# The MLP's down projection as 2x2 blocks with seven block products, with two weight sums made in DRAM

## The chip, the cores and the metric

The kernel runs on one core of a Trainium2 chip. The metric is the device time of one execution in microseconds, from the first instruction to the end. The profile's span is the time from the first to the last instruction of one profiled execution.

## The reference

One layer of an encoder on 512 tokens of width 2048, all in float32. Its last step is the one that changes:

```python
h = x
xn = rmsnorm(h);  y = xn @ W_in
h += concat[gdn(y[:, :4112]), rwkv7(y[:, 4112:])] @ W_out   # 8 heads x 128, 16 heads x 64
h += cross_attention(rmsnorm(h), rmsnorm(mem))              # 4 heads, 256 memory tokens
h += (max(rmsnorm(h) @ W_up, 0) ** 2) @ W_down              # 2048 -> 8192 -> 2048
out = rmsnorm_final(h)
```

## The kernel before

Activations are kept transposed: channels on the 128 partitions, the 512 tokens along the free axis. `hres[n]` (n = 0 to 15) is the residual's tile of 128 channels x 512 tokens. A float32 product is made of three fast ones: an operand x is split into `hi`, x rounded by a cast on ScalarE (ACT, L130), and `lo` = x - `hi` on VectorE (DVE, L131), and hi x hi, hi x lo and lo x hi are added up in PSUM. So each weight tile of 128x1024 is loaded by SP's queue (`wraw`), cast by ACT (`whi`), subtracted by DVE (`wlo`) and used by 24 matmuls on TensorE (PE).

The stages in order: the input projection (`py`), head pair by head pair, with the two recurrences of each pair (RWKV-7 tiles have names such as `ri`, `rs`; GDN tiles `gi`, `gs`); the output projection; the cross attention (`kp`, `vp`, `kq`, `vo`, `sc`, `at`, `op`); up; down; the last normalisation.

GpSimd (POOL) works in the first part only. For each pair of heads it inverts small triangular matrices by substitution, one diagonal at a time, in two chains: `sr` for RWKV-7 (64 partitions, from a MEMSET of `sr` to a COPY of `sr`) and `sgi`/`sgj` for GDN (32 partitions, to a COPY of `sgi`). SP's queue stores each result to DRAM (`bg16T<-sr`, `bg8T<-sgi`) and reads it back in another layout (`r`, `E`, `gk`, `gqn`). The same queue, in the same order, loads the projection's weights (`wraw<-in_w_in`).

The order of the first part is set by a scheduler in the program: operations of the projection and of the recurrences (whose line in the profile is L247) are merged by estimated times. The order in each engine's queue is fixed when the kernel is built, and each engine and each queue issues in order. An instruction that waits holds up what stands behind it.

Up (W_up, 2048 x 8192) is computed in 32 steps `p` as 2x2 blocks with seven block products each (Strassen's scheme in Winograd's form) in place of eight. The activations' seven combinations (`comb`, tiles `cb_`) are made once ahead of it. Each step loads four weight tiles, makes four weight sums on DVE, and has seven products of 24 matmuls with 256 columns (half the tokens). The sums of products are made on DVE (L1438). `square` (L1537, L1538) applies the squared ReLU; two transfers per step, issued by ACT, put the result u into DRAM (`Ud`).

Down (W_down, 8192 x 2048) is plain: eight slabs `e` of 1024 rows of W_down; for each slab 16 output tiles `n`, each with one weight tile and 24 matmuls of 512 columns, `dn`, added into `hres[n]` by DVE (L1559). Pieces of u are read back (`usplit`) and split one slab ahead. The last slab goes by halves of the tokens (`last`), so that the normalisation of the first half runs beside the products of the second; `scaled` (L1583) multiplies and stores.

Of the kernel before, what the change touches and what calls it, by code (L numbers as in the profile page):

```python
# [73 lines left out]
def build(tc, I, out):  # L74
# [267 lines left out]
    VOd = [pd.tile([P, 8, 512], F32, name=f"vod{i}", tag=f"vod{i}") for i in range(4)]  # L342

# [881 lines left out]
    hres = [ph.tile([P, T], F32, tag=f"h{k}", name=f"h{k}", bufs=1) for k in range(16)]  # L1225
# [159 lines left out]
    def put(i, k, src):  # L1385
        t = comb[i][k]
        S.copy(t[:, HA], src)
        V.tensor_tensor(out=t[:, HB], in0=src, in1=t[:, HA].bitcast(F32), op=ALU.subtract)

    def sub(o, a, b):  # L1390
        V.tensor_tensor(out=o, in0=a, in1=b, op=ALU.subtract)

    def place(i, k, e, o):


        if i == T1:
            sub(e[:, HA], e[:, HB], e[:, HA])
        elif i == T2:
            sub(e[:, HA], o[:, HB], e[:, HA])
        elif i == T3:  # L1400
            sub(e[:, HB], o[:, HB], e[:, HB])
        elif i == T4:
            sub(e[:, HA], e[:, HA], o[:, HA])
        put(i, k, o[:, HB] if i == B22 else o[:, HA] if i == B21 else e[:, HB] if i == T3 else e[:, HA])

    def strassen(nm, pool, src, ks, done, used=None, first=False):

        w = len(ks) * P

        def raw(p_, tag, bufs, i):
            cnt[0] += 1
            r = p_.tile([P, 1024], F32, tag=tag, name=f"{tag}_{cnt[0]}", bufs=bufs)[:, 0:w] \
                if p_ is pw else p_.tile([P, pool[1]], F32, tag=tag, name=f"{tag}_{cnt[0]}", bufs=bufs)[:, 0:w]
            if i is not None:
                nc.sync.dma_start(r, src[i])
            return r

        def product(i, tag, a):
            cnt[0] += 1
            hi = pw.tile([P, 1024], F32R, tag="whi", name=f"whi{cnt[0]}", bufs=NWS)[:, 0:w]
            lo = pw.tile([P, 1024], F32R, tag="wlo", name=f"wlo{cnt[0]}", bufs=NWS)[:, 0:w]
            split(a, hi, lo)
            pt = psb(f"{nm}_{i}", tag)[:, 0:M]
            for z, k in enumerate(ks):
                sl = slice(z * P, z * P + P)
                mm(pt, hi[:, sl], comb[i][k][:, HA], start=z == 0, stop=False)
                mm(pt, hi[:, sl], comb[i][k][:, HB], start=False, stop=False)  # L1430
            for z, k in enumerate(ks):
                mm(pt, lo[:, z * P:z * P + P], comb[i][k][:, HA], start=False, stop=z == len(ks) - 1)
            if used:
                used(i)
            return pt

        def add(o, a, b, op=ALU.add):
            V.tensor_tensor(out=o, in0=a, in1=b, op=op)  # L1438

        def wraw2(i):  # L1440
            return raw(pool[0], "wraw2", 3, i)

        def ws():
            return raw(pool[0], "ws", 2, None)

        a11 = raw(pw, "wraw", NWR, 0)
        if first:
            a12, a22 = raw(pw, "wraw", NWR, 3), raw(pw, "wraw", NWR, 2)
            a21 = wraw2(1)
        else:  # L1450
            a21 = raw(pw, "wraw", NWR, 1)
            a22, a12 = wraw2(2), wraw2(3)
        p1 = product(B11, "mx", a11)
        c1 = sl2()
        c11, c12 = u1, u4 = c1[:, HA], c1[:, HB]
        S.copy(u1, p1)
        if first:
            p2 = product(B21, "mg", a12)
            p4 = product(T4, "mx", a22)
        s1 = ws()  # L1460
        add(s1, a21, a22)
        p5 = product(T1, "mg", s1)
        s2 = ws()
        add(s2, s1, a11, ALU.subtract)
        p6 = product(T2, "mm", s2)
        c2 = sl2()
        c21, c22 = u3, u2 = c2[:, HA], c2[:, HB]
        add(u2, u1, p6)
        if first:
            add(c11, u1, p2)  # L1470
        add(u4, u2, p5)
        add(a21, a11, a21, ALU.subtract)
        p7 = product(T3, "mm", a21)
        add(u3, u2, p7)
        add(c22, u3, p5)
        done(1, HB, c2)
        if not first:
            p4 = product(T4, "mx", a22)
        add(c21, u3, p4, ALU.subtract)
        done(1, HA, c2)  # L1480
        s4 = ws()
        add(s4, a12, s2, ALU.subtract)
        p3 = product(B22, "mg", s4)
        add(c12, u4, p3)
        done(0, HB, c1)
        if not first:
            p2 = product(B21, "mm", a12)
            add(c11, u1, p2)
        done(0, HA, c1)
# [3 lines left out]
    for n in range(KD):  # L1493
# [9 lines left out]
        if n % 2 == 0 and n < KD - 2:  # L1503
            for i in (B11, T1):
                place(i, n // 2, ge, None)
        elif n % 2 == 1:
            for i in range(2, 7) if n < KD - 2 else (B11, T1, B21, T2, T4, T3, B22):
                place(i, n // 2, ge, g)
# [3 lines left out]
    Ud = [pd.tile([P, 2, 512], F32, name=f"ud{i}", tag=f"ud{i}") for i in range(32)]  # L1512
    pu_cm = tc.tile_pool(name="pu", bufs=1, reuse_waits="tile")
    pu = pu_cm.__enter__()
    uhl = [], []

    def usplit(f):
        if f >= 8:
            r = sl2()
        elif f % 2:  # L1520
            r = ph.tile([P, T], F32, tag="acc", name=f"ur{f}", bufs=1)
        else:
            r = pu.tile([P, T], F32, tag="ur", name=f"ur{f}", bufs=1)
        nc.sync.dma_start(r, Ud[f // 2][:, f % 2, :])
        hi, lo = act_tile(f"uh{f}"), act_tile(f"ul{f}")
        if f < 56:
            split(r, hi, lo)
        else:
            for t, half in ((hi, HA), (lo, HB)):
                split(r[:, half], t[:, HA], t[:, HB])  # L1530
        uhl[0].append(hi)
        uhl[1].append(lo)

    for p in range(32):
        def square(i, half, c):
            t = c[:, half]
            V.scalar_tensor_tensor(out=t, in0=t, scalar=0.0, in1=rstd[:, half], op0=ALU.max, op1=ALU.mult)  # L1537
            S.activation(t, t, AF.Square)  # L1538
            if half is HA:
                nc.scalar.dma_start(Ud[p][:, i, :], c)  # L1540

        def used(i):
            if p == 0 and i == B21:
                pt = psb("pss2")
                mm(pt, ones, acc)
                rsq(rstd, pt, 1.0 / 2048, b_eps6)
            if p == 31 and i in (T1, T2, T3):
                for f in (range(0, 3), range(3, 6), range(6, 8))[i - T1]:
                    usplit(f)

        strassen(f"up{p}", (pu, 1024), [I["w_up"][p, i] for i in range(4)], list(range(8)), square, used, p == 0)
    for e in range(7):
        uh, ul = uhl[0][e * 8:], uhl[1][e * 8:]
        for n in range(KD):
            if n % 2 == 0:
                usplit(e * 8 + 8 + n // 2)
            pt = psb(f"dn{e}_{n}", "mm", 2)
            gemm(pt, I["w_dn"][e, n], 8, uh, ul)
            V.tensor_tensor(out=hres[n], in0=hres[n], in1=pt, op=ALU.add)  # L1559


    def last(n, half, wide):

        pt = psb(f"dn7_{n}", "mm", 2)
        wh, wl = wload(I["w_dn"][7, n])
        u = uhl[half is HB][56:]
        h = hres[n][:, half]
        for k in range(8):
            sl = slice(k * P, k * P + P)
            if wide:  # L1570
                mm(pt, wh[:, sl], u[k], start=k == 0, stop=False)
            else:
                mm(pt[:, HA], wh[:, sl], u[k][:, HA], start=k == 0, stop=False)
                mm(pt[:, HA], wh[:, sl], u[k][:, HB], start=False, stop=False)
            mm(pt[:, HA], wl[:, sl], u[k][:, HA], start=False, stop=k == 7)
        V.tensor_tensor(out=h, in0=h, in1=pt[:, HA], op=ALU.add)
        if wide:
            V.tensor_tensor(out=h, in0=h, in1=pt[:, HB], op=ALU.add)

    acc = ph.tile([P, T], F32, tag="acc", name="acc3", bufs=1)  # L1580
# [6 lines left out]
    ready = []  # L1587
    for half in (HA, HB):
        for n in range(KD):
            last(n, half, half is HA or n < KD - 1)  # L1590
            sq = acc[:, half] if n == 0 else sl2(M)
            S.activation(sq, hres[n][:, half], AF.Square)
            if 0 < n < KD - 1:
                V.tensor_tensor(out=acc[:, half], in0=acc[:, half], in1=sq, op=ALU.add)
            for _ in range(2 if 1 < n < 5 else n > 1):
                if ready:
                    scaled(ready.pop(0), HA)
        pt = psb("pss3")[:, HA]
# [108 lines left out]
```

## Time and profile before

| | us |
|---|---|
| median of 3 runs (range) | 3058.04 (3057.87 to 3059.95) |
| span of the profiled execution | 3053.3 |
| the median above that span | 4.7 |
| PE busy | 3022.5 |
| PEld (weight loads of PE, beside it) busy | 2607.5 |
| DVE busy | 1916.1 |
| ACT busy | 1355.4 |
| POOL busy | 216.3 |

The page does not give the profiled execution's whole time, only its span; the median of the runs stands for it. The DMA queues moved 403.14 MB, 132 GB/s as a mean. In rows of the profile, L12 is a line of the kernel, `out<-in` are the names of tiles without their numbers, and what stands in brackets behind a row, or behind an arrow, is what ended the wait ahead of it. SPq and ACTq are transfers issued by SP and ACT.

### The profile page before, as it was taken

To read this page: it belongs to the slowest core of one execution; us is meant where nothing else is said; L and a number is where in the kernel's file an instruction comes from. 1 tells how busy PE (TensorE), PEld (TensorE's weight loads), DVE (VectorE), ACT (ScalarE), POOL (GpSimd) and SP (SyncE) were. 2 spreads that over 40 slices of the span, in tenths; PEclk is the share of its full clock that TensorE was granted. 3 is DMA by queue.
4 is the path that set the end of the run, shared out by engine and by line. 5 is a ranking of instruction groups with operands and counts; after the bars stand their busy time and mean duration, and the time that the engine had idled before them with its cause. 6 is when DMAs were issued, how large, how long until landed. Compare 5 with 4: busy or idle time off the path is not lost.

```text
span 3053.3 us, 50831 instructions
## 1 busy us (share of the span) xinstructions
PE 3022.5 (99%) x20740; PEld 2607.5 (85%) x20740; DVE 1916.1 (63%) x2881; ACT 1355.4 (44%) x1864; POOL 216.3 (7%) x547
## 2 busy tenths in 40 slices
PE   9999999999999999999999999999999999999998
PEld 7888878878878898778878999999999888888887
DVE  7666666666677647534348888888887443444457
ACT  6455455455555555533336544444444222222234
POOL 0312311312312000000000000000000000000000
PEclk9999999999999999999999999999999999999999
DMA  5322322323425586753323433333334332333335
GB/s 186 104 80 80 108 80 80 108 80 87 135 73 162 172 272 231 262 201 122 110 92 90 142 130 130 132 132 135 125 135 163 124 118 104 125 125 125 113 130 180
DMA packets 226746, 403.14 MB, mean 132 GB/s; under 512 B 91656, under 2 KB 115468, under 8 KB 226512
## 3 DMA queue, kind: packets, MB, share of 16 engines
q1 hardware_dynamic: 210384, 372.62, 37.5%
q10 hardware_dynamic: 16128, 27.27, 2.4%
q8 instruction: 163, 2.67, 0.3%
q14 instruction: 71, 0.58, 0.1%
HBM read 352.23 MB, written 47.59 MB: 131 GB/s over the span
## 4 chain that ended last, share of the span: by engine, by line
PE 95%; DVE 1%; ACT 1%; DMA 1%; issue 1%; POOL 0%; SPq 0%; DVEq 0%; ACTq 0%; POOLq 0%
PE dn L122 23%; PE up L122 21%; PE py L247 21%; PE op L122 6%; PE vp L122 3%; PE sc L122 3%; PE at L122 3%; PE kq L247 3%; PE vo L122 3%; PE kp L247 2%; PE rs L247 1%; PE gs L247 1%; PE pgB L247 1%; PE po L247 0%; PE gpo L247 0%
## 5 line engine op out<-in xcount | busy, mean ns | idle before, releaser
L130 ACT CAST whi<-wraw 128x1024 fp32r<-128x1024 f32 x384 | 403.6, 1051 | 814.3 <-PE dn L122 474.8
L131 DVE TENSOR_TENSOR wlo<-wraw,whi 128x1024 fp32r<-128x1024 f32 x384 | 469.7, 1223 | 135.6 <-ACT whi L130 131.5
L122 PE MATMUL up<-cb,whi 128*128 128x256 f32 x3584 | 467.4, 283 | 1.3 <-ACT whi L130 0.7
L122 PEld LDWEIGHTS up<-cb,whi 128*128 128x128 f32 x3584 | 446.3, 192 | 2.4 <-ACT whi L130 1.7
L122 PE MATMUL dn<-ul,whi 128*128 128x512 f32 (+1 forms) x1032 | 395.0, 389 | 0.9 <-ACT whi L130 0.9
L122 PE MATMUL dn<-uh,whi 128*128 128x512 f32 x1024 | 393.8, 390 | 0.0
L122 PE MATMUL dn<-uh,wlo 128*128 128x512 f32 (+1 forms) x1024 | 384.5, 375 | 0.0
L247 PE MATMUL py<-xhi,whi 128*128 128x512 f32 x928 | 371.8, 401 | 6.1 <-ACT xhi L247 6.0
L247 PE MATMUL py<-xhi,wlo 128*128 128x512 f32 x928 | 371.7, 401 | 0.0
L247 PE MATMUL py<-xlo,whi 128*128 128x512 f32 x928 | 371.4, 400 | 0.3 <-DVE xlo L247 0.3
L247 DVE TENSOR_TENSOR wlo<-wraw,whi 128x1024 fp32r<-128x1024 f32 (+1 forms) x180 | 221.7, 1231 | 128.2 <-ACT whi L247 126.5
L1559 DVE TENSOR_TENSOR h<-h,dn 128x512 f32<-128x512 f32 x112 | 77.0, 688 | 331.1 <-PE dn L122 331.1
L247 ACT CAST whi<-wraw 128x1024 fp32r<-128x1024 f32 (+1 forms) x180 | 188.2, 1046 | 203.0 <-PE py L247 165.3
L122 PE MATMUL up<-cb,wlo 128*128 128x256 f32 x1792 | 251.5, 283 | 0.0
L122 PEld LDWEIGHTS up<-cb,wlo 128*128 128x128 f32 x1792 | 231.2, 192 | 0.0
L122 PEld LDWEIGHTS dn<-ul,whi 128*128 128x128 f32 x1032 | 193.9, 188 | 41.2 <-ACT whi L130 1.2
L122 PEld LDWEIGHTS dn<-uh,whi 128*128 128x128 f32 x1024 | 192.2, 188 | 40.9
L122 PEld LDWEIGHTS dn<-uh,wlo 128*128 128x128 f32 x1024 | 192.3, 188 | 35.0
L247 PEld LDWEIGHTS py<-xhi,whi 128*128 128x128 f32 x928 | 174.9, 188 | 41.2 <-ACT xhi L247 6.2
L247 PEld LDWEIGHTS py<-xlo,whi 128*128 128x128 f32 x928 | 174.9, 188 | 35.6 <-DVE xlo L247 1.4
L247 PEld LDWEIGHTS py<-xhi,wlo 128*128 128x128 f32 x928 | 174.9, 189 | 35.3 <-issue 1.0
L130 ACT CAST whi<-ws 128x1024 fp32r<-128x1024 f32 x96 | 100.5, 1047 | 150.8 <-PE up L122 93.9
(741 smaller groups left out, 5145.4 us busy)
## 6 DMA issues: line engine op xcount, KB each, us to landing
wraw<-in_w_dn SPq DMA_DIRECT2D x144, 512.0 KB, 3.5
wraw<-in_w_up SPq DMA_DIRECT2D x128, 512.0 KB, 3.5
wraw<-in_w_in SPq DMA_DIRECT2D x116, 512.0 KB, 3.6
wraw<-in_wk SPq DMA_DIRECT2D x32, 512.0 KB, 3.9
wraw<-in_wqT SPq DMA_DIRECT2D x32, 512.0 KB, 5.4
wraw<-in_wv SPq DMA_DIRECT2D x32, 512.0 KB, 4.6
wraw<-in_wo SPq DMA_DIRECT2D x32, 512.0 KB, 5.9
wraw<-in_w_out SPq DMA_DIRECT2D x32, 512.0 KB, 3.9
```

The source lines that it names most:

```text
L122: PE.matmul(o, l, r, start=start, stop=stop)
L130: S.copy(hi, src)
L131: V.tensor_tensor(out=lo, in0=src, in1=hi.bitcast(F32), op=ALU.subtract)
L247: f(*a, **k)
L1559: V.tensor_tensor(out=hres[n], in0=hres[n], in1=pt, op=ALU.add)
```

## The change

Down is now computed with seven block products too. W_down is cut into four chunks `c` of 2048 rows, each a 2x2 of blocks: A11, A21, A22, A12 for each pair of output tiles. Each chunk computes one product at a time over all eight half tiles `m`; a product's block is 24 matmuls of 256 columns (`block`, L1436 and L1439). Partial sums that two outputs share stay in PSUM: `X[a]` takes products 0, 3, 5 and 6, `y` products 2 and 4, and `z` product 1; `into` adds them, 512 columns at a time, into the residual, which now lies in tiles `hq`.

Up writes, in place of u, its seven combinations: u's four blocks and three differences, with four transfers per step into `Cd`. Up's own sums of products are partly made in PSUM now, with the signs of some combinations turned. `piece_` reads a piece of a combination back and splits it.

Of the weight sums that down needs, two (T2's and B22's) are made on DVE in SBUF. The other two, S1 = A22 + A21 and S3 = A11 + A21, are made in DRAM (`SUMS`): for each of 16 tiles, a GpSimd transfer copies one block (1.05 MB), and a second one adds the other to it as it writes. That is 64 transfers of 1.05 MB each, DRAM to DRAM. 224 weight tiles are loaded in down, 144 before.

The core of the diff:

```diff
+    SUMS = {i: [pd.tile([P, 2048], F32, name=f"ws{i}_{u}", tag=f"ws{i}_{u}") for u in range(16)] for i in (0, 1)}
+    Cd = [pd.tile([P, 7, 512], F32, name=f"cd{q}", tag=f"cd{q}") for q in range(16)]
...
+    for u in range(16):
+        for i, b in ((0, 2), (1, 0)):
+            GP.dma_start(SUMS[i][u], I["w_dn"][u, b])
+            GP.dma_start(SUMS[i][u], I["w_dn"][u, 1], accum_op=ALU.add, max_dma_last_dim=2048)
...
+    def block(pt, a, parts, start):
...
+        split(a, hi, lo)
+        for k in range(8):
+            for x in parts[k]:
+                PE.matmul(pt, hi[:, k * P:k * P + P], x, start=start, stop=False, skip_group_check=True)
+                start = False
+        for k in range(8):
+            PE.matmul(pt, lo[:, k * P:k * P + P], parts[k][0], start=False, stop=k == 7, skip_group_check=True)
...
         def used(i):
-            if p == 0 and i == B21:
-                pt = psb("pss2")
+            if p == 0 and i == T1:
+                pt = psb("pss2", "scr", 1)
                 mm(pt, ones, acc)
                 rsq(rstd, pt, 1.0 / 2048, b_eps6)
...
+        nc.scalar.dma_start(Cd[p // 2][:, 2:4, h], v(c2))
+        nc.scalar.dma_start(Cd[p // 2][:, 0:2, h], v(c1))
+        nc.scalar.dma_start(Cd[p // 2][:, 4:6, h], v(t))
+        nc.scalar.dma_start(Cd[p // 2][:, 6, h], t4)
...
-    for e in range(7):
-        uh, ul = uhl[0][e * 8:], uhl[1][e * 8:]
-        for n in range(KD):
-            if n % 2 == 0:
-                usplit(e * 8 + 8 + n // 2)
-            pt = psb(f"dn{e}_{n}", "mm", 2)
-            gemm(pt, I["w_dn"][e, n], 8, uh, ul)
-            V.tensor_tensor(out=hres[n], in0=hres[n], in1=pt, op=ALU.add)
...
+        for a in range(4):
+            y = psb(f"dy{c}_{a}", *TAGS[a])
+            ms = (2 * a, 2 * a + 1)
+            s1 = [raw(weights(c, m, S1)) for m in ms]
+            for m in ms:
+                down(c, 2, m, y, s1[m % 2], True)
+            into(a, OD, HB, y, ADD)
+            a11 = [raw(weights(c, m, A11)) for m in ms]
+            for m in ms:
+                add(s1[m % 2], s1[m % 2], a11[m % 2])
+                down(c, 3, m, X[a], s1[m % 2], False)
+            into(a, EV, HB, X[a], SUB)
...
+        for m in range(8):
+            down(c, 5, m, X[m // 2], raw(weights(c, m, S3)), False)
+            if m % 2:
+                into(m // 2, OD, HB, X[m // 2], ADD)
```

Where the sums in DRAM stand on POOL: at its start. Before the change its first memsets (`WTz`, `BTz`, `TtG`) were followed by the chain on `sr`:

```order
L247 MEMSET BTz 128x896
L247 MEMSET TtG 128x512
L247 MEMSET sr_980 64x256
L247 MEMSET sr_980 64x16
L247 ISA
L247 TENSOR_TENSOR gEs_1025<-gE_764,cst 128x512
L247 TENSOR_TENSOR sr_981<-sr_980 64x15
L247 TENSOR_TENSOR sr_980<-sr_980,sr_981 64x15
```

With the change the transfers (`ws_0` and on) follow these memsets, two copies and then two adding ones:

```order
L247 MEMSET BTz 128x896
L247 MEMSET TtG 128x512
L1308 DMA ws_0_120<-in_w_dn 16x16384
L1308 DMA ws_0_136<-in_w_dn 16x16384
L1309 DMA ws_0_120<-in_w_dn 512x512
L1309 DMA ws_0_136<-in_w_dn 512x512
L1308 DMA ws_1_121<-in_w_dn 16x16384
L1308 DMA ws_1_137<-in_w_dn 16x16384
```

32 of them stand ahead of the first chain's arithmetic. The other 32 stand between the chain's steps; this is its end, and the start of the second chain, on `sgi`:

```order
L247 TENSOR_TENSOR sr_1029<-sr_1028 64x15
L1308 DMA ws_15_135<-in_w_dn 16x16384
L247 TENSOR_TENSOR sr_1028<-sr_1028,sr_1029 64x15
L1308 DMA ws_15_151<-in_w_dn 16x16384
L247 COPY sr_1028<-sr_1028 64x256
L247 MEMSET sgi_1329 32x256
L1309 DMA ws_15_135<-in_w_dn 512x512
L247 MEMSET sgi_1329 32x16
L1309 DMA ws_15_151<-in_w_dn 512x512
L247 TENSOR_TENSOR sgj_1330<-sgi_1329 32x15
```

So all 64 stand ahead of the second chain, and 62 ahead of the COPY that ends the first. SP's queue and PE's rows in this part are the same as before.

On PE at the end of the cross attention (`at`) and the start of up, `pss`, the sum of squares over all tiles of `hres`, stood behind two blocks of products (`up_0`, `up_6`). Before, around the second block's end:

```order
L122 MATMUL up_6_16681<-cb_6_15860,wlo_16678 128x256
L122 MATMUL up_6_16681<-cb_7_16578,wlo_16678 128x256
L122 MATMUL pss_16706<-acc_15811,cst_74 128x512
L122 MATMUL up_4_16714<-cb_0_15840,whi_16710 128x256 x2
L122 MATMUL up_4_16714<-cb_1_15841,whi_16710 128x256 x2
```

With the change it stands ahead of the first block:

```order
L122 MATMUL at_16644<-plo_15226,whi_16647 128x512
L122 MATMUL at_16644<-phi_15218,wlo_16648 128x512
L122 MATMUL pss_16811<-acc_15915,cst_74 128x512
L1436 MATMUL upx_16719<-cb_0_15916,whi_16724 128x256 x2
L1436 MATMUL upx_16719<-cb_1_15917,whi_16724 128x256 x2
```

Two blocks of 24 matmuls that stood ahead of `pss` now stand behind it.

More of the change, by code (lines that the diff above doesn't have):

```diff
@@ L1400, in place @@
         elif i == T3:
-            sub(e[:, HB], o[:, HB], e[:, HB])
+            sub(e[:, HB], e[:, HB], o[:, HB])
         elif i == T4:
[L1403 to L1432, printed above, removed]
@@ L1433, in product, with strassen @@
+    def strassen(p, done, used):
+        def product(i, pt, a, start=True):
+            block(pt[:, HA], a, [(comb[i][k][:, HA], comb[i][k][:, HB]) for k in range(8)], start)
             if used:
                 used(i)
[L1435 to L1446, printed above, removed]
@@ L1479, in strassen @@
[L1479 to L1489, printed above, removed]
+        a11, a21, a22, a12 = (raw(I["w_up"][p, i]) for i in range(4))
+        s1 = raw(None)
+        x, y, z = (psb(f"up{n}{p}", t) for n, t in (("x", "mx"), ("y", "mg"), ("z", "mm")))
@@ L1580, in build, with later, into @@
-    acc = ph.tile([P, T], F32, tag="acc", name="acc3", bufs=1)
+                for q in ((0,), (1, 2), (3,))[i - T1]:
+                    piece_(0, 0, q)
+        strassen(p, square, used)
+    def later(n):
+        for _ in range(n):
+            if todo:
+                piece_(*todo.pop(0))
+    EV, OD = 0, 1
+    view = lambda t: t.rearrange("p (a b) -> p a b", b=M)
+    def into(a, par, half, pt, op):
+        h = hq[a][par][:, :, half]
+        V.tensor_tensor(out=h, in0=h, in1=view(pt), op=op)
@@ L1585, in scaled @@
         (nc.sync if n % 2 else nc.scalar).dma_start(out[n][:, half], h)
[L1587 to L1598, printed above, removed]
[L1599 to L1604 removed]
+    todo += [(0, i, q) for i in range(1, 7) for q in range(4)]
@@ L1605, in build @@
+    norm(HA, [sums["A"], sums["last"]])
     for n in range(KD):
-        scaled(n, HB)
+        scaled(n, HA)
     pu_cm.__exit__(None, None, None)
```

235 lines of the change are left out of this document (150 added, 85 removed).

## The prediction

> **What bounds the kernel now.** I read the page's busy times first, then its chain of the work that ended last. The third and fourth rows below are the busy share of the DMA engines, in tenths, and their GB/s, in 40 slices of the span.
>
> ```profile
> PE 3022.5 (99%) x20740; PEld 2607.5 (85%) x20740; DVE 1916.1 (63%) x2881; ACT 1355.4 (44%) x1864; POOL 216.3 (7%) x547
> PE 95%; DVE 1%; ACT 1%; DMA 1%; issue 1%; POOL 0%; SPq 0%; DVEq 0%; ACTq 0%; POOLq 0%
> DMA  5322322323425586753323433333334332333335
> GB/s 186 104 80 80 108 80 80 108 80 87 135 73 162 172 272 231 262 201 122 110 92 90 142 130 130 132 132 135 125 135 163 124 118 104 125 125 125 113 130 180
> ```
>
> TensorE is busy 99% of the span and is 95% of the chain, so whatever takes columns away from it should pay, and whatever makes it wait is paid in full. POOL is idle 93% of the time, but an average says nothing about the moments when TensorE needs POOL. So I looked at the stages one by one: a stretch's length, then busy time (and count) of PE, PEld, DVE, ACT and POOL, then the granted clock, the DMA share and GB/s.
>
> ```profile
> 0.00:76.30 76.30, 69.89 (x292) 54.78 (x293) 56.00 (x95) 53.27 (x77) 2.43 (x11) 1.00 0.53 186
> 76.30:152.70 76.40, 75.52 (x571) 61.59 (x571) 48.93 (x71) 35.44 (x48) 28.05 (x67) 1.00 0.37 105
> 1075.00:1100.00 25.00, 25.00 (x209) 25.00 (x209) 10.59 (x9) 13.28 (x18) 0.00 (x0) 1.00 0.85 274
> 1831.90:1908.20 76.30, 76.30 (x638) 76.30 (x638) 63.76 (x84) 34.01 (x46) 0.00 (x0) 1.00 0.38 131
> 2336.30:2943.00 606.70, 606.70 (x2678) 502.34 (x2677) 250.84 (x292) 152.17 (x179) 0.00 (x0) 1.00 0.35 122
> ```
>
> Up (the fourth) and down (the fifth) are TensorE without a gap, at full clock; DVE is at 84% in up and 41% in down. The third stretch is the busiest that I found for the DMA engines: 274 GB/s at a share of 0.85, so 274/0.85 = 322 GB/s would fill them. The first two hold POOL's work on the first heads.
>
> Two chains of waits (start, length, engine and tile) follow: first that of the end, then that of 100 to 200 us.
>
> ```profile
> 1708.29 628.07 PE up L122 x5232
> 2336.36 654.41 PE dn L122 x2943
> ...
> 2999.52 40.55 PE dn L122 x231
> 3040.10 0.43 DVE h L1576
> ```
>
> ```profile
> 147.02 0.62 POOL sgi L247
> 148.05 2.36 DMA E<-bg16U
> 151.12 0.83 PE ri0u L247 x30
> ```
>
> A matmul of 256 columns in up takes 628.07/5232 = 0.120 us. Down runs from 2336.36 to 3040.07: 703.7 us. The second chain matters as much. POOL's COPY of `sgi` at 147.02 releases SP's store of it, the transfer `E<-bg16U` stands behind that store on SP's queue, and TensorE waits for `E`. The slack there is nil already.
>
> **The change, part by part.**
>
> *Down's products.* 4 chunks x 7 products x 8 half tiles x 24 matmuls = 5376 matmuls of 256 columns, which is up's own count and shape, so 5376 x 0.120 = 645.1 us in place of 703.7: **-58.6 us**. Whether the feeders keep up I work out from these groups (by form; count, then busy us and mean ns), of up's stretch and of down's:
>
> ```profile
> L131 DVE TENSOR_TENSOR wlo<-wraw,whi 128x1024 fp32r<-128x1024 f32 x15 | 18.3, 1219 | 0.0
> L130 ACT CAST whi<-wraw 128x1024 fp32r<-128x1024 f32 x15 | 15.7, 1048 | 22.8 <-PE up L122 15.5 <-DVE sl L1438 7.3
> L1438 DVE TENSOR_TENSOR sl<-sl,up 128x256 f32<-128x256 f32 x27 | 11.3, 419 | 12.8 <-PE up L122 12.8
> L1438 DVE TENSOR_TENSOR ws<-wraw,wraw 128x1024 f32<-128x1024 f32 x4 | 4.9, 1224 | 0.1
> ```
>
> ```profile
> L1559 DVE TENSOR_TENSOR h<-h,dn 128x512 f32<-128x512 f32 x111 | 76.3, 688 | 327.8 <-PE dn L122 327.8
> L131 DVE TENSOR_TENSOR ul<-sl,uh 128x512 fp32r<-128x512 f32 x48 | 31.6, 689 | 8.9 <-ACT uh L130 8.6
> L130 ACT CAST uh<-sl 128x512 fp32r<-128x512 f32 x48 | 29.0, 620 | 16.3 <-DMA sl<-ud 15.9
> ```
>
> A chunk of down is 56 blocks of 24 matmuls, 161.3 us. DVE has 56 x 1.22 (weight splits) + 16 x 1.22 (the two weight sums made in SBUF) + 28 x 0.69 (into `hq`) + 28 x 0.69 (pieces of u) = 126.5 us, 78%. ACT has 56 x 1.05 + 28 x 0.62 = 76 us, 47%. The loads are 56 x 0.524 + 28 x 0.262 MB = 36.7 MB, 227 GB/s, 71% of 322. TensorE stays the bound. The cover is thinner than before (41% of DVE), so I allow for one late weight split (1.05 + 1.22 us) at two places: **+4 us**, between 0 and 9 (one for each of four chunks).
>
> *Up.* A `p` still takes 168 matmuls, 20.16 us. DVE has 7 x 1.22 + 4 x 1.22 + 7 x 0.42 + 2 x 0.69 = 17.7 us, 88% (84% before), and ACT issues four stores instead of two, with half its time free: nothing. At p = 0 the sum of squares `pss2` now stands ahead of the first block. It waits for the last add into `acc`, and the two blocks that ran meanwhile (2 x 24 x 0.120 = 5.8 us) no longer cover that: **+6 us**, between 0 and 6.
>
> *The tail.* The last normalisation, the scaling of half the columns and their stores are as before. The front's TensorE rows are the same too.
>
> Without the sums in DRAM this gives 3053.3 - 58.6 + 4 + 6 = 3004.7 us of span, against the profiled 3053.3.
>
> *The sums in DRAM.* In the program they stand after the attention, but nothing there holds them, and the rows of POOL in the section on the change show that they are placed in its queue at the start of the kernel. It works in order; each pair of accumulating transfers must wait until the pair of copies before it has landed. Here are POOL's rows of before around that place (start, length, operation, and the idle time ahead of it):
>
> ```profile
> 2.43 0.52 POOL L247 MEMSET TtG<- 128x512 f32 x1
> 84.65 0.48 POOL L247 MEMSET sr<- 64x256 f32 x2 [81.69 <-ACT whi L247]
> 103.43 1.30 POOL L247 TENSOR_TENSOR gEs<-gE,cst 128x512 f32<-128x512 f32 x1 [18.30 <-ACT gE L247]
> 118.09 0.61 POOL L247 COPY sr<-sr 64x256 f32<-64x256 f32 x1
> 130.98 0.21 POOL L247 TENSOR_TENSOR sgj<-sgi 32x15 f32<-32x15 f32 x1 [11.86 <-DMA sgi<-ndgi]
> 147.02 0.61 POOL L247 COPY sgi<-sgi 32x256 f32<-32x256 f32 x1
> ```
>
> All 64 transfers stand ahead of the chain that began at 130.98. What waits behind POOL is on SP's queue (start, issue time, transfer):
>
> ```profile
> 118.05 0.59 SPq L247 DMA_DIRECT2D bg16T<-sr  x1
> 121.68 0.33 SPq L247 DMA_DIRECT2D wraw<-in_w_in  x1
> 146.99 0.33 SPq L247 DMA_DIRECT2D bg8T<-sgi  x1
> 148.05 0.58 SPq L247 DMA_DIRECT2D E<-bg16U  x1
> 150.07 0.55 SPq L247 DMA_DIRECT2D wraw<-in_w_in  x1
> ```
>
> When SP waits for `sr` or `sgi`, the projection's weight loads wait behind it, so TensorE has no other work to take up. Let T be the time at which POOL has got through the 64 transfers.
> - Start: 3 us (the memset at 2.43).
> - 32 copies of 1.05 MB: 33.6 MB at 322 GB/s, 104 us. The trace has no transfer from DRAM to DRAM. The nearest row, a load, gives this; were the reading and the writing both to count, it would be 208.
> - 32 accumulating transfers: nothing of the kind in the trace either. They read two operands and write one, three passes where a copy has two: 1.5 x 104 = 156 us. Bounds: 104 (as a copy) and 312 (1.5 x 208). I take 156, on the load's row as for the copies.
> - The front's own loads use the same engines: 0.53 x 76.3 + 0.37 x 76.4 = 69 us of them.
> - Issue by POOL, and the time until a pair has landed: the trace has no transfer issued by POOL. SP's rows above give 0.33 to 0.59 us each, 21 to 38 us for 64, part of it beside moving data: 20, between 0 and 70 (the upper end with 2 us of landing for 16 pairs).
>
> T = 3 + 104 + 156 + 69 + 20 = 352 us. The second chain can't start at once: from the COPY of `sr` (118.09) to 130.98 it took 12.9 us, and that COPY leaves POOL one pair's landing (2.1 MB, 6.5 us) ahead of T, so 6 more. TensorE's loss is 352 + 6 - 131 = **+227 us**. Nothing hides it: TensorE waits for `E` already, and the weights of any other work stand behind SP's waits. After it the front runs on as before, since POOL has no transfers left.
>
> The sum: 3004.7 + 227 = 3231.7 us of span. The median of the three runs, 3058.04, lies 4.7 above the profiled span, so the **predicted time is 3236 us**.
>
> **The rivals.**
>
> *A. The transfers move faster than that.* If an accumulating one costs no more than a copy and issue hides, T = 280, loss 280 + 6 - 131 = 155, time 3009.4 + 155 = 3164. For it: the DMA row shows the engines mostly at 2 to 3 tenths. Against: the second operand has to be read. At the far end, 400 GB/s for all, T = 3 + 84 + 84 + 69 = 240: time 3124.
>
> *B. An accumulating transfer costs two copies.* 208 us in place of 156: 3288. By bytes I find no reason, by number of reads there is one. The Trainium skill, Collectives: The Full Stack, the section "The bandwidth ceiling: the fold count and why AG ≠ RS ≠ AR", states that an adding transfer runs at half a copying one's speed since both operands are read through the same ring of descriptors. No run here shows it; by that rule the time would be this rival's 3288.
>
> *C. DRAM to DRAM counts both ways, or POOL needs microseconds to issue one.* Up to T = 3 + 208 + 312 + 69 + 20 = 612: time 3009.4 + 487 = 3496. Halfway (T = 480) it is 3364. For it: writes and reads use one memory. Against: nothing in the trace moves that way.
>
> *D. POOL is through in time: faster.* Place: POOL's second chain, at 131 us before. Price: what it starts late. It decides at 58.6 - 4 - 6 = 48.6 us of lateness: if the 64 transfers are done by 131 + 49 - 6 = 174 us, the gain in down pays for them. Beside 69 us of loads that asks 67.1 MB in 102 us, 658 GB/s, twice the 322 of the busiest stretch. If the transfers cost nothing at all the time is 3009. For it: only that a store from POOL's first chains might not be waited for, and the chain of waits shows the opposite. That the change does not shorten down at all (TensorE starved there) would take another 58 us off the gain; up's stretch, with DVE at 84% and no gap, speaks against it.
>
> **How the numbers follow.** Chances: the forecast, 3190 to 3262, 0.40; A, 0.19 (0.04 of it below 3110); B, 3262 to 3320, 0.21; C, 0.15 (0.08 of it above 3420); D, 0.05. The range is 3110 to 3420, and leaves out 0.17. About 0.2% of the time, 6 us, is what a measurement of this kernel can tell from no change. Faster by more than that: 0.04 (D); within it: 0.02 (D's edge and A's far tail); slower: 0.94.
>
> **What would show it.** In the profile of the changed kernel: POOL's issues of `ws_` from about 3 us on, with long waits between pairs; the chain `sgj<-sgi` starting at about 358 us instead of 131; TensorE's busy share far below 9 tenths in the slices up to there, and the DMA row near 9; then slices as before, moved by 227 us. Down from its first matmul to its last in 645 to 657 us, PE at 9 tenths, and a wait of `pss` of some us at the start of up. I am wrong if TensorE's slices are full before 350 us (D), if the transfers' GB/s is far from 322 (A, C), or if down shows idle TensorE.

## The result, and the profile after

The changed kernel takes 3215.86 us (median of 4 runs, 3214.58 to 3217.7), the kernel before 3058.99 us beside it: a ratio of 1.0514, 95% interval 1.0499 to 1.0529. It is 157 us slower; 178 were forecast.

From the page of the changed kernel: busy times, the chain that ended last by engine and by line, the 40 slices of PE and of the DMA engines, and the queue of the transfers that POOL issues.

```profile
PE 2988.3 (93%) x22912; PEld 2679.7 (83%) x22912; DVE 2080.5 (65%) x2925; ACT 1482.7 (46%) x2000; POOL 259.9 (8%) x611
...
PE   6920799999999999999999999999999999999998
...
DMA  9999343233234256868432335444444677676754
...
q0 software_dynamic: 17920, 67.11, 8.4%
...
PE 82%; DMA 12%; DVE 2%; ACT 2%; issue 1%; POOL 1%; SPq 0%; POOLq 0%; DVEq 0%; ACTq 0%
PE py L247 17%; DMA ws<-in_w_dn 8%; PE upx L1436 7%; PE dx L1436 7%; PE op L122 5%; PE upy L1436 4%; PE upx L1439 4%; PE dy L1436 3%; PE dx L1439 3%; PE kq L247 3%; PE sc L122 3%; PE at L122 3%; PE vp L122 3%; PE kp L247 2%; PE vo L122 2%; PE upy L1439 2%
```

TensorE is busy for less time than before (2988.3 against 3022.5 us), yet the span is 160.8 us longer (3214.1 against 3053.3). The third and fourth slices, 160 to 320 us, are nearly empty on PE while the DMA engines are full; from the sixth slice on PE is full again. `ws<-in_w_dn`, the transfers that make the sums, are a link of the chain. The stretches of the front (columns as in the prediction):

```profile
0.00:76.30 76.30, 51.10 (x182) 37.66 (x183) 38.00 (x68) 34.41 (x50) 12.81 (x25) 0.87 1.02 301
76.30:152.70 76.40, 76.20 (x481) 60.94 (x480) 47.81 (x70) 43.85 (x60) 9.63 (x13) 1.00 1.05 269
152.70:229.00 76.30, 18.70 (x79) 14.81 (x77) 9.38 (x12) 7.75 (x9) 18.84 (x32) 0.64 0.99 252
229.00:300.00 71.00, 0.00 (x0) 0.00 (x0) 0.00 (x0) 0.00 (x0) 19.02 (x38) 0.50 1.01 244
```

POOL's own rows (start, length, operation, idle time ahead of it and what ended it), the first group of transfers, some late ones and the second chain:

```profile
2.91 1.17 POOL L1308 DMA_DIRECT2D ws<-in_w_dn  x2
11.61 1.07 POOL L1309 DMA_DIRECT2D ws<-in_w_dn  x1 [7.53 <-DMA ws<-in_w_dn]
...
243.90 1.06 POOL L1309 DMA_DIRECT2D ws<-in_w_dn  x1 [12.09 <-DMA ws<-in_w_dn]
...
312.38 1.07 POOL L1309 DMA_DIRECT2D ws<-in_w_dn  x1 [11.43 <-DMA ws<-in_w_dn]
...
314.96 1.03 POOL L1309 DMA_DIRECT2D ws<-in_w_dn  x1 [1.38 <-DMA ws<-in_w_dn]
332.33 0.20 POOL L247 TENSOR_TENSOR sgj<-sgi 32x15 f32<-32x15 f32 x1 [16.34 <-DMA sgi<-ndgi]
```

and SP's queue:

```profile
144.58 1.43 SPq L247 DMA_DIRECT2D lg<-in_g2a  x1
299.67 0.59 SPq L247 DMA_DIRECT2D bg16T<-sr  x1
...
346.49 0.58 SPq L247 DMA_DIRECT2D E<-bg16U  x1
```

POOL issues an adding transfer in 1.1 us, after it has stood 7.5 to 12 us in these rows until the copies ahead have landed. SP stands from 146 to 299.67 us, waiting to store `sr`, with the projection's weights behind. `E` is transferred at 346.49 instead of 148.05: 198.4 us late.

At the start of up, and from the last product of up to the first of down (timeline of PE), then two stretches of down and the last products (chain):

```profile
1891.44 2.08 PE L122 MATMUL pss<-acc,cst 128*128 128x512 f32 x2 [2.78 <-DVE acc L1304]
...
1901.54 2.18 PE L1436 MATMUL upy<-cb,whi 128*128 128x256 f32 x16 [1.64 <-ACT whi L130]
...
1905.58 2.17 PE L1436 MATMUL upx<-cb,whi 128*128 128x256 f32 x16 [0.90 <-ACT whi L130]
```

```profile
2544.06 0.28 PE L1436 MATMUL dx<-dh,whi 128*128 128x256 f32 x1
```

```profile
2544.06:2620.00 75.94, 70.21 (x569) 68.45 (x568) 60.52 (x75) 41.81 (x57) 0.00 (x0) 1.00 0.84 281
2620.00:2700.00 80.00, 80.00 (x668) 79.99 (x668) 65.35 (x71) 38.09 (x44) 0.00 (x0) 1.00 0.75 241
```

```profile
3198.06 0.97 PE dx L1439 x8
```

Down starts 2544.06 - 2336.36 = 207.7 us later than before: 198.4 in the front, 5.3 in the three waits at the start of up, and 4.0 that are not traced to a wait here. It then takes 3199.03 - 2544.06 = 655.0 us instead of 703.7, 48.7 less. What comes after it takes 15.1 us instead of 13.2. The sum, 207.7 - 48.7 + 1.9 = 160.9, is the whole difference of the spans.

### The profile page after: what moved, and what is told of

Same layout as the page of the kernel before. It is cut to its first block, busy times and chain, and to the rows that moved or that the text cites. A ratio compares the mean times of both kernels' runs of the same rounds, so it can differ in the third digit from the quotient of the medians.

```text
span 3214.1 us, 56104 instructions
## 1 busy us (share of the span) xinstructions
PE 2988.3 (93%) x22912; PEld 2679.7 (83%) x22912; DVE 2080.5 (65%) x2925; ACT 1482.7 (46%) x2000; POOL 259.9 (8%) x611
## 3 DMA queue, kind: packets, MB, share of 16 engines
q0 software_dynamic: 17920, 67.11, 8.4%
## 4 chain that ended last, share of the span: by engine, by line
PE 82%; DMA 12%; DVE 2%; ACT 2%; issue 1%; POOL 1%; SPq 0%; POOLq 0%; DVEq 0%; ACTq 0%
PE py L247 17%; DMA ws<-in_w_dn 8%; PE upx L1436 7%; PE dx L1436 7%; PE op L122 5%; PE upy L1436 4%; PE upx L1439 4%; PE dy L1436 3%; PE dx L1439 3%; PE kq L247 3%; PE sc L122 3%; PE at L122 3%; PE vp L122 3%; PE kp L247 2%; PE vo L122 2%; PE upy L1439 2%
## 5 line engine op out<-in xcount | busy, mean ns | idle before, releaser
L130 ACT CAST whi<-ub 128x1024 fp32r<-128x1024 f32 x260 | 272.3, 1048 | 291.0 <-PE dx L1436 68.6
L131 DVE TENSOR_TENSOR wlo<-ub,whi 128x1024 fp32r<-128x1024 f32 x260 | 317.6, 1222 | 87.6 <-ACT whi L130 87.3
L130 ACT CAST whi<-ua 128x1024 fp32r<-128x1024 f32 x188 | 197.0, 1048 | 210.5 <-PE dx L1436 55.2
L1436 PE MATMUL upx<-cb,whi 128*128 128x256 f32 x2048 | 268.3, 284 | 1.7 <-ACT whi L130 1.7
L131 DVE TENSOR_TENSOR wlo<-ua,whi 128x1024 fp32r<-128x1024 f32 x188 | 229.7, 1222 | 58.1 <-ACT whi L130 57.8
L1436 PEld LDWEIGHTS upx<-cb,whi 128*128 128x128 f32 x2048 | 255.8, 193 | 3.2 <-ACT whi L130 2.6
L1436 PE MATMUL dx<-dh,whi 128*128 128x256 f32 x1024 | 252.0, 284 | 2.2 <-ACT whi L130 2.0
L1436 PE MATMUL dx<-dl,whi 128*128 128x256 f32 x1024 | 251.2, 283 | 0.0
L131 DVE TENSOR_TENSOR wlo<-wraw,whi 128x1024 fp32r<-128x1024 f32 x112 | 137.2, 1225 | 112.1 <-ACT whi L130 111.1
L1436 PEld LDWEIGHTS dx<-dh,whi 128*128 128x128 f32 x1024 | 196.5, 192 | 3.2 <-ACT whi L130 3.0
L1436 PEld LDWEIGHTS dx<-dl,whi 128*128 128x128 f32 x1024 | 196.5, 192 | 0.0
L130 ACT CAST whi<-wraw 128x1024 fp32r<-128x1024 f32 x112 | 117.7, 1051 | 152.2 <-PE op L122 68.9
L1439 PE MATMUL upx<-cb,wlo 128*128 128x256 f32 x1024 | 143.7, 283 | 0.0
L1439 PE MATMUL dx<-dh,wlo 128*128 128x256 f32 x1024 | 143.7, 283 | 0.0
```

Of the source, the lines that this page charges most:

```text
L130: S.copy(hi, src)
L131: V.tensor_tensor(out=lo, in0=src, in1=hi.bitcast(F32), op=ALU.subtract)
L1436: PE.matmul(pt, hi[:, k * P:k * P + P], x, start=start, stop=False, skip_group_check=True)
L1439: PE.matmul(pt, lo[:, k * P:k * P + P], parts[k][0], start=False, stop=k == 7, skip_group_check=True)
```

## The experiments

The trace names POOL's order. The question was whether that order is the cause, or whether 67 MB from DRAM to DRAM cost this much wherever they run. "Sums" are the 64 transfers; ratios are to the kernel before on the same chip, with their 95% intervals.

**No sums.** What is the rest of the change worth?

```diff
-            GP.dma_start(SUMS[i][u], ...)            # all 64
-        src = SUMS[b - 4][u] if b >= 4 else I["w_dn"][u, b]
+        src = I["w_dn"][u, (2, 0)[b - 4] if b >= 4 else b]
```

> The 64 transfers of the sums are left out; the products that used S1 and S3 load A22 and A11 in their place, so the two sums are missing from the result. Everything else is as in the changed kernel. Theory 'queue' (the front's 200 us are POOL's second chain standing behind the 64 transfers; the rest of the change is worth 703.7 - 655.0 = 49 us in down, less 7 at the start of up and 2 at the end): 3059 - 40 = 3019 us, within 5, and the front as before (transfer of E at about 148 us). Rival 'other costs' (part of the 200 us comes from something else of the change): clearly above 3030 us.

Measured: 3013.89 us, 0.9865 (0.985 to 0.9879), 41 us faster than before, with `E` transferred at 150.05 us. The whole loss, 6.5% or 198 us, is that of the sums. All ratios below are read against this 0.9865.

**The sums alone**, added to the kernel before:

> The kernel before, with 64 transfers of the same shapes and order of kinds added, whose results nothing uses; up and down are untouched. They stand wholly ahead of POOL's first chain here, so that this chain's 14 us and the 13 us from it to the second one come after them too. Theory 'queue': second chain at about 315 + 14 + 13 = 342 us in place of 131, so 3059 + 211 = 3270 us, within 15. Rival 'other costs': less than 3059 + 150 = 3209 us.

Measured: 3256.27 us, 1.0658 (1.064 to 1.0676), 201 us more; the second chain starts at 331.52 us, 10 earlier than expected, and the time is within the expected 15. The two parts of the change add up: -41 and about +200.

**The sums elsewhere.** Issued in up behind a small POOL copy of `rstd`, and issued right behind POOL's last work on the recurrences:

```diff
+                gate = GP.tensor_copy(gt, rstd[:, 0:64])     # in up, behind rsq at p == 0
+                with tc.issue_after(gate.ins):
+                    ...                                      # the loop over the 64 transfers
```

> The same 64 transfers, issued by POOL behind a small copy of rstd at the start of up, where POOL has no other work (about 1690 us). Theory 'queue': nothing waits behind POOL, up has half of its DMA time free (share 0.50), the sums are ready some 300 us later and well ahead of down: 3019 to 3026 us. Rival 'traffic' (67 MB from DRAM to DRAM cost their engine time wherever they run, since they take it from the loads): above 3100 us.

> The same 64 transfers, right behind POOL's last operation of the recurrences (about 965 us), so that they run beside the output projection and the first half of the attention, where the loads alone take 0.7 to 0.84 of the DMA engines. Theory 'queue': POOL holds up nothing; what is lost is only what the loads lose there, between 0 and 140 us (if each side gets half of the engines while both want them): 3020 to 3160 us, waits on loads of in_wk, in_wv, in_wqT or in_wo. Rival 'traffic': as far up as in the changed kernel, about 3216 us.

Measured: 3093.43 us in up, 1.0120 (1.0101 to 1.0139); 3167.68 us behind the recurrences, 1.0365 (1.0349 to 1.038). Nothing waits behind POOL there, and still the sums cost 78 and 153 us. The theory that only the queue matters missed both, and so did the rival (above 3100, and about 3216). Behind the recurrences the DMA engines are full from 960 to 1350 us (shares of 0.99 to 1.06), and TensorE waits there for weights of the attention. DMA issues of the run in up, first while the transfers run (1700 to 2080 us), then after them (2100 to 2400): count, KB, median us from issue to landing.

```profile
ub<-in_w_up SPq DMA_DIRECT2D x34, 512.0 KB, 8.4
...
cd<-tt ACTq DMA_DIRECT2D x15, 256.0 KB, 11.1
```

```profile
ub<-in_w_up SPq DMA_DIRECT2D x33, 512.0 KB, 4.3
...
cd<-tt ACTq DMA_DIRECT2D x15, 256.0 KB, 5.2
```

Beside the sums the loads and stores take about twice as long, though up leaves half of the engines' time free (a DMA share of 0.47 without the sums). TensorE's largest wait in up (us in total, times, longest):

```profile
PE upz L1432 <- ACT whi L130: 49.8, 11, 8.8
```

The waits are not all of it. From 1700 to 2080 us the granted clock is 0.87 to 0.96, 1.00 in the run without sums, and a matmul takes 0.129 us of TensorE's busy time instead of 0.120: 23 us more for the 2551 in that stretch. With the 49.8 us this is about the 71 us by which this execution (3084.52 us) lies above the run without sums.

**The traffic without the waits.** Eight plain copies at the same place, the same bytes, and no sums; then the same with rows of 4 KB:

```diff
+    for j in range(8):
+        GP.dma_start(spare[j], I["w_dn"][2 * j:2 * j + 2]...)   # 128x16384; later max_dma_last_dim=4096
```

> As the run without the sums (the two sums are missing from the result), and at the place where the changed kernel has its 64 transfers POOL issues 8 plain copies from DRAM to DRAM of 8.4 MB each, the same 67.1 MB, into memory that nothing uses; none of them waits, so POOL's chains run as before. It has the traffic in the front without the waits. Theory 'queue' (the 200 us are POOL's order; traffic alone costs TensorE what it cost in up, some 17% of the time that it lasts): 0.987 of before and 30 to 60 us more, so a ratio of 0.997 to 1.007. Rival 'traffic' (the loads beside 67 MB cost the 200 us by themselves, and POOL's waits only hide behind it): a ratio of 1.04 to 1.055.

Measured: 3214.53 us, 1.0521 (1.0506 to 1.0537), the figure of the changed kernel without one transfer on POOL that waits. The rival was right about this run. Its queue, a stretch of its front, SP's issues, and two of SP's waits up to 250 us (us in total, times, longest):

```profile
q0 software_dynamic: 1152, 67.11, 6.0%
```

```profile
40.00:80.00 40.00, 0.00 (x0) 0.00 (x0) 0.00 (x0) 0.00 (x0) 0.00 (x0) 0.50 0.98 334
```

```profile
32.33 0.33 SPq L247 DMA_DIRECT2D gEG<-in_xT  x1
59.56 0.33 SPq L247 DMA_DIRECT2D gqd<-in_xT  x1
85.89 0.33 SPq L247 DMA_DIRECT2D lw<-in_w2a  x1
```

```profile
SPq L247 <- DMA wraw<-in_w_in: 83.2, 5, 27.5
SPq L247 <- DMA gv<-in_xT: 26.0, 1, 26.0
```

67.11 MB in 1152 packets are 58 KB each. While they move, SP gets on by one transfer in 26 us, as one of its earlier loads lands, and this is so for 256 KB in rows of 2 KB (`gv`) as for 512 KB in rows of 4 KB (`wraw`). Either is 128 rows, 8 for each of 16 engines; a row of 64 KB takes an engine 65.5 KB / (334 GB/s / 16) = 3.1 us; 8 turns of 3.1 us are 25 us. That fits engines which take turns between queues row by row, not byte by byte. The Trainium skill, DMA: Bandwidth & Descriptors, the section "SWDGE vs HWDGE vs iDMA", has the engines take turns between the queues that feed them, with packets, preferably of at most 4096 B, as the boundary; these rows agree with the turns, with packets of 58 KB. From it came two more theories to test: rows of 4 KB here, in the sums in up, and in the changed kernel itself.

> The run with 8 plain copies of 8.4 MB at the front and no sums (the two sums are missing from the result), with those copies cut into rows of 4 KB. The same traffic in the front, without waits and without long rows. Theory 'queue and long rows, each enough by itself': loads get their turn, and the ratio falls from 1.052 to between 0.987 (the one without sums) and 1.005. Rival 'bytes': it stays above 1.04. If POOL itself takes long to write so many rows, or its ring is full, its chains start late, and the ratio lies between.

> The run with the sums in up again, with the copies cut into rows of 4 KB (256x1024) in place of 64 KB (16x16384); the adding transfers have rows of 2 KB as before. Bytes, order and waits are the same. Theory 'long rows' (the engines take turns between queues row by row: a weight load's 4 KB row waits for a whole 64 KB row of a copy, about 3.2 us on one engine at 20 GB/s, so loads and stores land late): weight loads of up land in 4 to 6 us in place of 8.4, the waits of up's products go down from 50 us to a few, and the ratio from 1.012 to 0.987 to 0.993. Rival 'bytes' (a share of the engines is taken whatever the rows): the ratio stays within 0.005 of 1.012.

> The changed kernel with the copies cut into rows of 4 KB, all 64 transfers still at the front of POOL's queue and with their waits. Theory 'queue' (POOL's second chain behind the 64 transfers is enough for the loss, whatever the rows are): TensorE runs fuller in the first 150 us, then stands still until the second chain as before; a ratio of 1.040 to 1.053, with E transferred at 310 to 350 us. Rival 'long rows alone' (without starved loads POOL's order costs little): below 1.02.

```diff
-            GP.dma_start(SUMS[i][u], I["w_dn"][u, b])
+            GP.dma_start(SUMS[i][u], I["w_dn"][u, b], max_dma_last_dim=4096)
```

Measured, with 64 KB and with 4 KB rows of the copies:

| | 64 KB | 4 KB (95%) |
|---|---|---|
| copies at the front, no waits | 1.0521 | 1.0266 (1.0251 to 1.0282) |
| sums in up | 1.0120 | 1.0067 (1.0052 to 1.0082) |
| sums at the front, with waits | 1.0514 | 1.0525 (1.0508 to 1.0543) |

Short rows help where nothing waits for POOL, but give back only part: the traffic in the front still costs 122 us, and in up 62, so both expectations on it missed, and so did their rivals, the one in up by 0.0003. In the front (4 KB rows) POOL has issued its eight copies by 45 us, so its own issuing is not what is late. Yet its second chain starts at 256.24 us instead of 130.98. Five small transfers, which follow one another, stand out in the chain of waits:

```profile
126.43 22.60 DMA ndri<-GB
149.10 22.64 DMA sr<-ndri
...
183.27 23.21 DMA bg16T<-sr
...
211.25 27.69 DMA ndgi<-gEs
238.96 17.14 DMA sgi<-ndgi
```

Together they take 113 us. In the kernel before, the medians of the five are 2.6 to 4.7 us each.

With the waits, short rows change nothing, as expected; `E` is transferred at 346.64 us. TensorE does get more in the first stretch, and then stands as long as before:

```profile
0.00:76.30 76.30, 56.32 (x197) 42.12 (x198) 39.72 (x70) 36.66 (x53) 13.26 (x25) 0.89 1.02 303
...
229.00:300.00 71.00, 0.00 (x0) 0.00 (x0) 0.00 (x0) 0.00 (x0) 20.41 (x41) 0.50 1.02 244
```

So in the front the traffic is enough without POOL's order (waits gone: 122 to 200 us), and with POOL's order the length of the rows makes no difference (waits kept: the same 200 us). No run holds POOL up without the traffic, so that the order alone would be enough is read from the trace and not tested. Both ways end at the same place: `E` is transferred 201 and 117 us later than without sums in the two runs with copies alone, and 196 and 197 in the two with waits, within about 5 us of what each loses.

**The adding transfers as plain ones**:

> The changed kernel with the second transfer of each sum a plain copy too (it overwrites the first, so the sums are missing from the result); number of transfers, waits and order as they are. Theory 'an adding transfer costs 1.5 to 1.6 copies': the period of a group of four, 16.8 us where nothing runs beside it, becomes 2 x 6.5 = 13 us, POOL is through some 55 to 65 us earlier, and the ratio falls from 1.051 to about 1.032. Rival 'an adding transfer costs no more than a copy': 1.051 again. Rival 'it costs two copies or more': the period falls to 11.2 us or less, a ratio of 1.022 or less.

Measured: 3181.5 us, 1.0414 (1.0397 to 1.0431), at none of the three figures. A group of four takes 13.6 us, the mean of five between 211.74 and 279.64 us; the last line is that stretch:

```profile
148.18 0.30 POOL L247 MEMSET sr<- 64x256 f32 x1 [52.11 <-ACT whi L247]
...
211.74 0.55 POOL L1309 DMA_DIRECT2D ws<-in_w_dn  x1 [8.85 <-DMA ws<-in_w_dn]
...
279.64 0.49 POOL L1309 DMA_DIRECT2D ws<-in_w_dn  x1 [7.01 <-DMA ws<-in_w_dn]
```

```profile
211.74:279.64 67.90, 0.00 (x0) 0.00 (x0) 0.00 (x0) 0.00 (x0) 16.37 (x42) 0.50 0.91 309
```

In the changed kernel it is 17.1 us (four groups from 243.90 to 312.38). If two copies take 6.8 us in both, two adding transfers take 17.1 - 6.8 = 10.3: 1.51 copies each. But the engines are busy only 0.91 of this stretch of plain copies (1.01 in the changed kernel's, 243.90 to 312.38), so copies alone need less than 6.8, and 1.51 is the low end. The run with rows of 4 KB, whose group takes 16.9 us, shows the two kinds apart; GB/s in 40 slices from 228 to 312 us:

```profile
GB/s 210 160 206 207 205 215 417 410 180 166 208 206 206 221 420 412 160 157 208 205 207 222 412 406 181 160 206 204 209 217 411 415 173 161 198 205 210 207 386 391
```

About 206 GB/s while adding transfers move, about 411 while copies do: that would be two copies. A stream of copies alone (rows of 64 KB) moved at 334 GB/s, which gives 1.6. So an adding transfer costs between 1.5 and 2 copies, and no run settles it further; the adding ones also have the shorter rows (2 KB), which the run with plain second transfers dropped with the adding. The time fell less than expected because POOL stood 52 us for its own MEMSET of `sr` between the transfers, until a weight cast in the front was done: T, the time at which POOL is through, fell by only 32 us, to 283, `E` was transferred at 310.07, and the time, by the ratios, fell by 31.

**Pacing in up**, one copy and one adding transfer a step, behind a copy of the step's result:

```diff
+        gate = GP.tensor_copy(gt, c1[:, 0:64])               # at the end of each step
+        with tc.issue_after(gate.ins):
+            GP.dma_start(SUMS[i][u], I["w_dn"][u, (2, 0)[i]])
+            GP.dma_start(..., accum_op=ALU.add, ...)         # the copy of the step before
```

> The 64 transfers in up again, but one copy and one adding transfer per step of up (20.16 us), each pair behind a small POOL copy that reads the step's result, in place of four in flight all the time: 2.1 MB per 20 us, 104 GB/s beside up's 150. Theory 'burst' (the transfers cost time in up because four are always in flight and take half of the engines, so that weights land late): the waits of up's products fall to a few us, and the ratio comes within 0.003 of the 0.987 without the sums. Rival 'bytes' (each MB from DRAM to DRAM costs the same wherever it runs): the ratio stays at the 1.012 of the sums in up.

Measured: 3247.44 us, 1.0634 (1.0615 to 1.0652), the worst of the four places, and neither theory holds. The largest wait, and the chain at one step:

```profile
PE upz L1432 <- ACT whi L130: 161.0, 26, 8.3
```

```profile
1822.34 10.24 DMA cd<-sl
...
1832.92 1.06 ACT whi L130
...
1834.03 3.78 PE upz L1432 x16
```

The pair now starts just as ACT stores the step's result. The store takes 10.2 us, ACT waits for its buffer, and the weight cast behind ACT's copy is late by some 6 us in each of 26 steps. The 16 matmuls behind that wait then take 3.78 us, 16 of the same shape a little later 1.92; the granted clock from 1700 to 2500 us is 0.86 to 0.89. Fewer transfers in flight did not help: they were put where a store was waited for. Another place in the step was not tried, nor was the second half of the attention, where the DMA share is 0.32 before the change (1374 to 1603 us).

**No sums in DRAM**: both blocks are loaded, and added in SBUF, by POOL and then by DVE.

```diff
+    def summed(c, m, b):
+        t, a21 = raw(weights(c, m, b)), raw(weights(c, m, A21))
+        GP.tensor_tensor(out=t, in0=t, in1=a21, op=ALU.add)   # then: add(t, t, a21), on DVE
+        return t
```

> No sums in DRAM: down loads both blocks of each sum, and POOL, idle there, adds them in SBUF just ahead of use (64 adds of 128x1024, about 2.6 us each by its 1.30 us for 128x512). Down's loads grow by 33.5 MB, from 224 to 275 GB/s, where 322 fill the engines. Theory 'queue': no transfer stands in POOL's front; the ratio is the 0.987 without the sums plus 0 to 15 us: 0.987 to 0.992. Rival 'down runs out of DMA or buffers': waits of dx and dy on weight casts, and a ratio above 0.995.

Measured: 3079.04 us, 1.0075 (1.006 to 1.009), a miss. Groups of its down by form (2400 to 3000 us):

```profile
L131 DVE TENSOR_TENSOR wlo<-ua,whi 128x1024 fp32r<-128x1024 f32 x83 | 123.7, 1492 | 19.7 <-ACT whi L130 19.5 <-PE dy L1433 0.2
L131 DVE TENSOR_TENSOR dl<-sl,dh 128x512 fp32r<-128x512 f32 x60 | 69.4, 1162 | 17.4 <-ACT dh L130 16.9
```

DVE's split takes 1.49 us here, 1.22 before. The Trainium skill, SBUF — State Buffer, the section "Who interferes with whom", says that a DVE operation with two inputs in SBUF and a GpSimd operation that reads SBUF contend, under an exclusive lock; these rows agree. The last run asks whether POOL's adds or the added loads were the price.

> No sums in DRAM: down loads both blocks of each sum and DVE adds them (64 more adds of 128x1024, 78 us over down, which has 655 us and some 490 us of DVE work; for the products with S3 alone DVE has 1.22 + 1.22 + 0.35 + 0.69 = 3.48 us per block of 2.88). Against the run in which POOL made these adds it keeps the loads (33.5 MB more) and takes POOL away. Theory 'POOL and DVE hinder each other' (the weight splits took 1.45 to 1.49 us beside POOL's adds, 1.22 without): splits back at 1.22 us, DVE late by up to 5 us in each of four chunks, a ratio between 0.987 and 0.994, faster than the kernel before. Rival 'down runs out of DMA or weight buffers' (what held down was the loading of two blocks): a ratio above 1.002, with waits on loads as there.

Measured: 3030.72 us against 3054.07, 0.9922 (0.9909 to 0.9936), as expected. The split is back at its length:

```profile
L131 DVE TENSOR_TENSOR wlo<-ub,whi 128x1024 fp32r<-128x1024 f32 x120 | 146.2, 1220 | 14.6 <-ACT whi L130 14.5
```

So the added loads and adds cost 17 us against the run without sums, and giving the adds to POOL 47 more. How much of the 47 is DVE's slower splits and how much that POOL's adds take 2.75 us each, where DVE's take 1.22, is not separated. This version computes the whole reference, and is faster than both kernels, by 23 us than the one before.

## Why the prediction was right, point by point

The queues of the changed kernel from 0 to 315 us, for the second point (packets, MB, share of 16 engines): first the transfers that POOL issues, then those that SP issues.

```profile
q0 software_dynamic: 16895, 65.08, 82.3%
q1 hardware_dynamic: 11616, 18.60, 19.7%
```

- *The bound, and the place of the loss.* TensorE is the bound but for the front, and the loss lies where it was put: POOL's second chain started at 332.33 us instead of 130.98, and TensorE stood still. Forecast was 358.
- *T, the time at which POOL is through the 64 transfers*, was 315 us, not 352. The moving was right: 6.5 + 9.75 = 16.25 us were forecast for a group of four, 17.1 measured, and 82.3% of 315 us is 259, where 260 were forecast. The loads took 19.7%, 62 us, not 69; TensorE fell behind, and the front had asked for fewer by then. The two shares leave no time over, so the 20 us for issue and landing, put on top, were mis-sized: they lie beside moving data. The last two adding transfers, some 10 us, move behind T.
- *From T to the second chain* it took 17 us, not 6: in the trace, the store of `sr` and the transfers to `sgi` queued beside these last sums. With this the front's term was 198 us to the transfer of `E`, in place of 227.
- *Down* gave 48.7 us, not 54.6. The products' time was right (5376 x 0.120 = 645.1); the loss beside it was 10 us, not 4, most of it in the first 76 us of down, where the DMA share is 0.84 and TensorE is busy 70.2 of 75.9 us. The chain of waits there goes largely through `sl<-cd`, the pieces of u that are read back (3.9 to 6.0 us each), and not through DVE, on which the term was sized.
- *The start of up* was sized rightly: 5.3 us in the three waits shown. *The tail* was put at nothing and cost 1.9.
- *The rivals.* The time lies in the forecast's own range, on A's side (3164). A's reason, an adding transfer at the price of a copy, is wrong: a group takes 17.1 us with adding transfers and 13.6 with plain ones. B's price, 13 us for two adding transfers, is too high (10.3), but its ratio of two copies is not excluded. The half speed of the Trainium skill, Collectives: The Full Stack, the section "The bandwidth ceiling: the fold count and why AG ≠ RS ≠ AR", is stated for another path; here 206 against 411 GB/s fit it, and 10.3 against 6.8 us do not. C's reason is wrong: copies alone moved 334 GB/s with the engines full, so reading and writing do not both count, and POOL issues a transfer in 0.5 to 1.1 us. D did not happen.
- *What the prediction lacked.* It costed the traffic as a share of the engines inside T and gave it no price of its own beside POOL's wait. Without any transfer that waits on POOL the same bytes cost 122 to 200 us in the front, and in up, with half of the engines free, 62 to 78. In this kernel's trace POOL's order ends the wait; removing it alone does not remove the loss. That the copies without waits lose the same 200 us as the order does is a coincidence as far as the runs show: nothing in them ties the two figures. At all four places that were tried the sums in DRAM cost more than the 41 us that down gains; that came only out of the runs.

## What to carry to other kernels

See where an instruction lands in its engine's queue, not where it stands in the program: a transfer that waits for another holds up all that follows on its issuing engine, and whoever waits for that. Cost an added bulk transfer by what it does to the landing time of the small loads and stores that others wait for; free bandwidth on average says little. When a change bundles a gain with a price, run it without the priced part first: here 0.9865 showed at once that the seven products gain 41 us and that the whole loss is that of the sums.

## What was not expected of the hardware

- Queues get their turns by rows: beside copies with rows of 64 KB, SP's loads landed one in some 26 us, about 3 us for each of the 8 rows on an engine, whether these had 2 or 4 KB.
- An adding transfer from DRAM to DRAM costs more than a copy, between 1.5 times (10.3 against 6.8 us for 2.1 MB) and twice (206 against 411 GB/s); which, no run settles.
- A wait of TensorE costs more than its length: behind one of 6 us, 16 matmuls took 3.78 us instead of 1.92, at a granted clock below 1.00 in these stretches.
- POOL's adds of 128x1024 made DVE's weight split slower, from 1.22 to 1.45 to 1.49 us, and the 512-wide one from 0.69 to 1.16.
- The 62 us that the sums in up still cost with 4 KB rows are 38 us of waits for weight casts and about 23 of slower matmuls (granted clock 0.91 to 0.95). What is not settled is why loads landed in 7.2 to 7.6 us instead of 4.3: how much of that is the share of the engines, how much the adding transfers' 2 KB rows, and how much memory that reads and writes at once, no run separates.
